# Two layers of a three-branch decoder trunk: the instruction order taken from the framework's other timing model

## The chip, the core and the metric

One core of a Trainium2 chip. The metric is device time in microseconds (us) of one execution. The core has five engines, each with a queue of its own: TensorE (PE in the profile, with its weight loads as PEld), VectorE (DVE), ScalarE (ACT), GpSimd (POOL), and SyncE (SP), which here only starts transfers. Each engine takes its instructions in the order of its queue; semaphores hold an instruction back until what it reads is written and what it overwrites has been read.

## What is computed

Two layers on a sequence of 512 tokens, width 1024, in fp32, and a final RMSNorm. Cut to what matters:

```python
def hybrid_layer(x, ...):
    h = rmsnorm(x, norm_g)
    proj = h @ w_in                       # 1024 x 8704: aq ak av az | u,v bz | cq ck cv cz | three gates
    ya = rmsnorm(diff_attention(rope(aq), rope(ak), av, lam), subln_g) * (1 - lam_init) * silu(az)
    uv = gelu(buv);  vb = layernorm(second half of uv)
    yb = u * (w_causal mixes vb over chunks of 128 + sgu_b) * silu(bz)
    yc = (softmax-weighted sum of three dilated windows of rope(cq), rope(ck), cv) * silu(cz)
    merged = sum over the branches of sigmoid(gate_n) * (y_n @ w_branch[n])
    return x + merged @ w_out
```

## The kernel before

**Arithmetic.** Every large product is made of three: weights and activations are each split into a rounded part ("hi") and the rest ("lo"), and TensorE adds hi x hi, lo x hi and hi x lo (lines 416 to 418, 439 to 441 and 452 to 454). Activations lie as tiles of 128 channels x 512 tokens. Some pairs of projections are made with seven products of half the length in place of eight (`seven`), for which sums and differences of weights are formed first (lines 178 to 181).

**Weights.** SyncE loads them in pieces of 128 x 1024 (`raw`, two buffers, line 140; a piece is loaded when an older one has been split). ScalarE rounds each half piece to `whi` (line 158, six buffers), and VectorE, or for each fifth half piece GpSimd, subtracts to get `wlo` (line 159, five buffers):

```python
        with tc.high_priority(offset=PRIO):
            A.activation(out=hi, in_=src, func=AF.Copy)
            (G if made[0] % LOMOD == 0 else V).tensor_tensor(out=lo, in0=src, in1=hi.bitcast(F32), op=ALU.subtract)
```

**Stages of a layer.** The head: products for `vb` (line 596 evicts them) and for A's values `va` (four PSUM banks, evicted by ScalarE, line 705), while VectorE scales x (line 585), splits it (`xh`, `xl`, line 422) and forms the mixed activations `mh`, `ml` (lines 505 to 508, split at 421 and 422). Then attention A and attention C, with other projections laid between their steps by hand (`fill`). Each q and k goes through `rope`: a VectorE shuffle (468) and product (469), a GpSimd product (470) and sum (471), a ScalarE rounding (732, 742) and a VectorE subtraction (733, 743). Each z is a SiLU: ScalarE's tanh (479) and a VectorE product (480). Then gates and branch products (`gl2`, `pb`), then the output product; its tail runs into the head of the next layer, or into the final norm.

**What sets the order.** The kernel's text gives each instruction a place; the splitting of weights is moved 300 places ahead by `high_priority`. When the tile framework closes its context, a list scheduler plays the whole program against a model of the core: whenever an engine is free in the model, it gets the ready instruction with the earliest place, and tile buffers are handed out as the model frees them. The order in which the model took the instructions becomes the order of each queue. Two such models exist, and the flag in the diff selects between them: a timeline of device occupancy (flag on), and the timing of the framework's functional simulator (flag off, the default). They differ in what they charge for instructions, transfers and semaphores; the program that they are given is the same. In the order that the first of them gave to the kernel before, 5508 of the 6605 instructions on TensorE's queue can be picked out as one run in written order; on VectorE's it is 747 of 1990, on ScalarE's 763 of 1662.

## Time and profile before

| | |
|---|---|
| time, median of 3 runs (lowest, highest) | 1154.71 us (1150.01, 1156.02) |
| the profiled execution: its own time | 1154.14 us |
| the profiled execution: span, first to last instruction | 1152.4 us |
| mean granted TensorE clock | 0.986 of full |
| busy: PE, PEld, DVE, ACT, POOL | 95%, 85%, 74%, 55%, 46% of the span |
| moved by DMA | 106.01 MB, mean 92 GB/s |

The profile is of one execution. Busy time is the time in which an engine's records lie; a matmul's record is longer than the distance to the next one's start, so a queue of matmuls reads as fully busy. Idle time is put down to the instruction that ended it. The span is 1.7 us shorter than the time of the same execution.

### The profile page before, as it was taken

How to read it: one execution, taken by the hardware profiler on the slowest of the kernel's cores; microseconds unless marked ns; L12 is line 12 of the kernel's file. 1: busy time of each engine (PE TensorE's matmuls, PEld its weight loads, DVE VectorE, ACT ScalarE, POOL GpSimd, SP SyncE). 2: the span in 40 equal slices, each digit the busy share in tenths (PEclk: the TensorE clock that was granted, in tenths of full speed). 3: DMA queues.
4: the chain of work that ended last, by engine and by line, in shares of the span. 5: the costliest groups of instructions: out<-in, count | busy, mean ns of one | idle time of the engine just before them, and what ended most of it. 6: DMA issues, size and time to landing. Idle time of an engine off the chain costs nothing.

```text
span 1152.4 us, 18434 instructions
## 1 busy us (share of the span) xinstructions
PE 1095.6 (95%) x6604; PEld 974.6 (85%) x6604; DVE 856.6 (74%) x1589; ACT 632.3 (55%) x1349; POOL 531.3 (46%) x503
## 2 busy tenths in 40 slices
PE   7898989999999999999997999899999999999977
PEld 5777879988888999988886888898888899999866
DVE  5796988667869887874569778857787887887533
ACT  5645666577865444443455475756777544544321
POOL 7653443235334667563342444323344456766312
PEclk9999999999999999999998999999999999999998
DMA  5221412220313333333622231313132233333333
GB/s 202 71 92 37 128 55 75 74 78 33 119 47 92 103 98 94 110 101 126 214 79 85 74 100 47 95 54 96 51 92 74 73 94 108 94 110 90 122 92 101
DMA packets 35643, 106.01 MB, mean 92 GB/s; under 512 B 4768, under 2 KB 8864, under 8 KB 35552
## 3 DMA queue, kind: packets, MB, share of 16 engines
q1 hardware_dynamic: 29936, 98.50, 27.5%
q10 hardware_dynamic: 5616, 6.34, 1.8%
q8 instruction: 52, 0.85, 0.3%
q14 instruction: 39, 0.32, 0.1%
HBM read 100.57 MB, written 4.24 MB: 91 GB/s over the span
## 4 chain that ended last, share of the span: by engine, by line
PE 68%; DVE 9%; issue 3%; DMA 2%; POOL 2%; ACT 2%; POOLq 0%; DVEq 0%; ACTq 0%; SPq 0%
PE ps_pj L416 11%; PE ps_pj L417 11%; PE ps_pj L418 11%; PE ps_to L416 7%; PE ps_to L418 7%; PE ps_to L417 7%; DVE wlo L159 2%; PE ps_to L898 2%; PE ps_to L1000 2%; DMA raw<-in_wpack 2%; PE ps_s L864 1%; PE ps_s L866 1%; PE ps_pj L441 1%; PE ps_pj L440 1%; PE ps_pj L439 1%
## 5 line engine op out<-in xcount | busy, mean ns | idle before, releaser
L158 ACT ACTIVATE whi<-raw 128x512 fp32r<-128x512 f32 x314 | 191.4, 626 | 225.8 <-DMA raw<-in_wpack 136.6
L159 DVE TENSOR_TENSOR wlo<-raw,whi 128x512 fp32r<-128x512 f32 x251 | 210.0, 844 | 88.1 <-ACT whi L158 44.2
L416 PE MATMUL ps_pj<-xh,whi 128*128 128x512 f32 (+1 forms) x544 | 208.4, 383 | 16.2 <-DVE z L480 7.1
L417 PE MATMUL ps_pj<-xl,whi 128*128 128x512 f32 (+1 forms) x544 | 205.3, 377 | 0.0
L418 PE MATMUL ps_pj<-xh,wlo 128*128 128x512 f32 (+1 forms) x544 | 204.4, 376 | 0.0
L159 POOL TENSOR_TENSOR wlo<-raw,whi 128x512 fp32r<-128x512 f32 x63 | 88.6, 1406 | 156.7 <-ACT whi L158 48.6
L416 PEld LDWEIGHTS ps_pj<-xh,whi 128*128 128x128 f32 x544 | 103.5, 190 | 35.6 <-DVE z L480 8.1
L418 PEld LDWEIGHTS ps_pj<-xh,wlo 128*128 128x128 f32 x544 | 103.6, 191 | 16.4
L417 PEld LDWEIGHTS ps_pj<-xl,whi 128*128 128x128 f32 x544 | 103.8, 191 | 15.6
L159 DVE TENSOR_TENSOR wlo<-t,whi 128x512 fp32r<-128x512 f32 x90 | 90.0, 1020 | 13.9 <-ACT whi L158 12.1
L158 ACT ACTIVATE whi<-t 128x512 fp32r<-128x512 f32 x112 | 64.8, 622 | 57.7 <-DVE t L179 29.6
L416 PE MATMUL ps_to<-mh,whi 128*128 128x256 f32 x320 | 91.0, 284 | 2.4 <-DVE zs L537 1.5
L417 PE MATMUL ps_to<-ml,whi 128*128 128x256 f32 x320 | 90.4, 283 | 0.0
L418 PE MATMUL ps_to<-mh,wlo 128*128 128x256 f32 x320 | 89.9, 283 | 0.2 <-DVE wlo L159 0.2
L470 POOL TENSOR_TENSOR rsh<-rsh,sinr 128x512 f32<-128x512 f32 x32 | 42.2, 1319 | 100.1 <-DVE rsh L468 100.1
L875 ACT ACTIVATE pr<-pr,nm 128x128 f32<-128x128 f32 (+3 forms) x128 | 71.0, 556 | 27.1 <-DVE nm L871 26.7
L871 DVE CUSTOM_DVE_ANT_0 pr<-ps_s,tab 128x128 f32<-128x128 f32 (+3 forms) x128 | 58.7, 483 | 14.7 <-PE ps_s L866 11.1
L416 PE MATMUL ps_to<-xh,whi 128*128 128x256 f32 x240 | 67.9, 283 | 0.4 <-ACT whi L158 0.4
L417 PE MATMUL ps_to<-xl,whi 128*128 128x256 f32 x240 | 67.9, 283 | 0.0
L418 PE MATMUL ps_to<-xh,wlo 128*128 128x256 f32 x240 | 67.8, 283 | 0.0
L416 PEld LDWEIGHTS ps_to<-mh,whi 128*128 128x128 f32 x320 | 61.3, 192 | 3.7 <-DVE zs L537 2.2
L790 POOL TENSOR_TENSOR acc<-acc,zs 128x512 f32<-128x512 f32 x32 | 51.0, 1601 | 23.3 <-DVE zs L789 19.5
(264 smaller groups left out, 3155.3 us busy)
## 6 DMA issues: line engine op xcount, KB each, us to landing
raw<-in_wpack SPq DMA_DIRECT2D x174, 512.0 KB
xf<-in_xT SPq DMA_DIRECT2D x8, 256.0 KB
xr<-in_xT ACTq DMA_DIRECT2D x8, 256.0 KB
x1d<-xf SPq DMA_DIRECT2D x8, 256.0 KB
xr<-x1d ACTq DMA_DIRECT2D x16, 128.0 KB
raw<-in_wpack SPq DMA_DIRECT2D x4, 256.0 KB
out<-xf SPq DMA_DIRECT2D x8, 128.0 KB
out<-xf ACTq DMA_DIRECT2D x8, 128.0 KB
```

Source lines behind the costliest of these rows:

```text
L158: A.activation(out=hi, in_=src, func=AF.Copy)
L159: (G if made[0] % LOMOD == 0 else V).tensor_tensor(out=lo, in0=src, in1=hi.bitcast(F32), op=ALU.subtract)
L416: T.matmul(ps, lhsT=wh, rhs=mh, start=first, stop=False)
L417: T.matmul(ps, lhsT=wh, rhs=ml, start=False, stop=False)
L418: T.matmul(ps, lhsT=wl, rhs=mh, start=False, stop=last)
L439: T.matmul(ps, lhsT=mh[:, ts], rhs=wh, start=kc == 0, stop=False)
L470: G.tensor_tensor(out=sh, in0=sh, in1=sinr, op=ALU.mult)
L790: G.tensor_tensor(out=acc[d], in0=acc[d], in1=th, op=ALU.add)
L871: V.tensor_tensor_reduce(out=pr[:, m, :W], in0=pss[m][:, :W], in1=tab[:, 0 if br == BR_A else 1, S - W :], op0=ALU.add, op1=ALU.min, scale ...
L875: A.activation(out=pr[:, m, :W], in_=pr[:, m, :W], func=AF.Exp, scale=-1.0, bias=nm[:, m : m + 1], accum_out=den[:, m : m + 1],)
L898: T.transpose(pt[:, j, :], pr[:, m, j * P : (j + 1) * P], ident)
L1000: T.matmul(po_[m][:, c], lhsT=v[:, j, 2 * h + m, :], rhs=pt[:, j, :], start=j + s_ == 0, stop=j == i and s_ == 1,)
```

## The change

The flag that selects the planner's timing model is turned off. No instruction, tile, buffer count, tensor or transfer in the kernel's text is changed; what may change is the order of the instructions on each queue, the buffer of a tag that each tile gets, and the semaphore waits that follow from both.

```diff
@@ -1132,7 +1132,7 @@
     args.append(nc.dram_tensor("out_0", (KC, P, S), F32, kind="ExternalOutput").ap())
-    with _tile.TileContext(nc, schedule_with_timeline_sim=True) as tc:
+    with _tile.TileContext(nc, schedule_with_timeline_sim=False) as tc:
         hybrid_kernel(tc, *args)
```

## Rows read from the trace of the kernel before

**Rows 1.** The page's head and its busy times by engine.

```profile
span 1152.4 us, 18434 instructions
PE 1095.6 (95%) x6604; PEld 974.6 (85%) x6604; DVE 856.6 (74%) x1589; ACT 632.3 (55%) x1349; POOL 531.3 (46%) x503
```

**Rows 2.** Windows by stage: stretch, length, busy PE PEld DVE ACT POOL, clock, DMA.

```profile
0.00:60.00 60.00, 48.73 (x186) 39.14 (x187) 38.89 (x63) 36.83 (x64) 43.24 (x68) 0.92 0.43 138
60.00:192.00 132.00, 121.99 (x650) 104.42 (x650) 114.38 (x246) 76.61 (x180) 58.16 (x50) 0.97 0.25 77
192.00:384.00 192.00, 188.46 (x1179) 168.32 (x1179) 146.58 (x306) 126.06 (x286) 73.70 (x87) 1.00 0.23 72
384.00:576.00 192.00, 190.59 (x1191) 172.66 (x1190) 138.90 (x189) 86.47 (x160) 108.05 (x76) 1.00 0.40 124
576.00:632.00 56.00, 49.66 (x212) 40.41 (x212) 44.90 (x63) 29.72 (x52) 19.66 (x14) 0.94 0.28 86
632.00:912.00 280.00, 274.28 (x1643) 242.24 (x1642) 210.50 (x488) 185.11 (x433) 110.41 (x120) 1.00 0.24 75
912.00:1086.00 174.00, 172.13 (x1170) 159.71 (x1170) 137.86 (x188) 77.98 (x148) 104.81 (x75) 1.00 0.34 104
1086.00:1152.00 66.00, 49.77 (x385) 47.73 (x383) 24.59 (x50) 13.49 (x29) 13.28 (x16) 0.93 0.30 93
```

**Rows 3.** Timeline of ScalarE at the head of layer 1: start, length, instruction.

```profile
625.32 0.63 ACT L421 ACTIVATE mh<-tm 128x512 fp32r<-128x512 f32 x1 [1.09 <-POOL tm L508]
625.86 0.67 ACT L705 ACTIVATE va<-ps_pj,rp 128x512 f32<-128x512 f32 x1
```

**Rows 4.** Timeline of TensorE there, ahead of its stop and behind it.

```profile
612.14 0.39 PE L453 MATMUL ps_pj<-whi,xul 128*128 128x512 f32 x1
...
612.37 0.39 PE L454 MATMUL ps_pj<-wlo,xuh 128*128 128x512 f32 x1
...
626.58 0.80 PE L416 MATMUL ps_pj<-xh,whi 128*128 128x512 f32 x1 [6.34 <-ACT va L705]
...
627.17 0.63 PE L417 MATMUL ps_pj<-xl,whi 128*128 128x512 f32 x1
627.60 0.63 PE L418 MATMUL ps_pj<-xh,wlo 128*128 128x512 f32 x1
```

**Rows 5.** Waits: who for whom, us in total, times, longest us.

```profile
ACT whi L158 <- DMA raw<-in_wpack: 136.6, 71, 8.4
POOL rsh L470 <- DVE rsh L468: 100.1, 25, 10.4
...
PE ps_pj L416 <- DVE z L480: 7.1, 3, 3.0
```

**Rows 6.** Groups by line and shape: busy us, mean ns, idle before.

```profile
L471 POOL TENSOR_TENSOR t<-t,rsh 128x512 f32<-128x512 f32 x30 | 41.5, 1382 | 2.9 <-DVE rd L880 1.4
L470 POOL TENSOR_TENSOR rsh<-rsh,sinr 128x512 f32<-128x512 f32 x32 | 42.2, 1319 | 100.1 <-DVE rsh L468 100.1
L732 ACT ACTIVATE q<-t 64x512 fp32r<-64x512 f32 x32 | 20.2, 631 | 11.8 <-POOL t L471 11.4
L178 POOL TENSOR_TENSOR t<-raw 128x512 f32<-128x512 f32 x28 | 37.4, 1336 | 35.2 <-DMA raw<-in_wpack 28.1 <-PE ps_to L898 6.9
```

**Rows 7.** Windows of line 471 alone, by stage: stretch, busy POOL, clock, DMA.

```profile
60.00:192.00 132.00, 11.29 (x8) 0.97 0.25 77
192.00:384.00 192.00, 10.36 (x8) 1.00 0.23 72
...
632.00:912.00 280.00, 22.41 (x16) 1.00 0.24 75
```

**Rows 8.** Windows of 4 us: a place with short stops, then the stop above.

```profile
80.00:84.00 4.00, 3.30 (x15) 2.47 (x14) 3.97 (x7) 0.22 (x1) 1.85 (x3) 1.00 0.32 67
...
624.00:628.00 4.00, 1.42 (x3) 1.17 (x4) 4.00 (x8) 2.61 (x6) 2.09 (x2) 0.51 0.45 131
628.00:632.00 4.00, 4.00 (x13) 3.21 (x12) 3.35 (x7) 1.77 (x5) 0.77 (x2) 0.64 0.43 131
```

**Rows 9.** Queue waits of SyncE: who for whom, us in total, times, longest us.

```profile
SPq L140 <- DVE wlo L159: 593.9, 108, 15.6
```

## Prediction

> **What bounds the kernel now.** I began with the page's head, to see which engine is near its limit, then took windows by stage, to see where that engine stops, and then the waits and the timeline at the largest stops.
>
> TensorE's records cover 1095.6 of the 1152.4 us, VectorE's 856.6 [rows 1]. The flag changes none of that work: the same matmuls have to pass, so an order can only give or take the time in which TensorE stands still or runs slowly. By stage [rows 2], TensorE stops for 11.3 us in the first 60 us (60 less 48.73) and for 16.2 us in the last 66 (66 less 49.77): the first loads, and the last products with the norm behind them. In between it stops for 10.0 + 3.5 + 1.4 + 6.3 + 5.7 + 1.9 = 28.8 us, in the order of the rows. The granted clock is below 1.00 in two of those stages: 0.97 over 132 us and 0.94 over 56 us, which is worth at most 4.0 + 3.4 = 7.4 us. So 36 us is all that an order can win between the ends.
>
> VectorE is the engine that TensorE waits behind when it waits. Its idle time in the same six stages is 17.6 + 45.4 + 53.1 + 11.1 + 69.5 + 36.1 = 232.8 us [rows 2]. It is 87% busy from 60 to 192 us, the tightest place, and 72 to 80% in the others.
>
> What a planner's order can do wrong is to be seen at the head of layer 1. TensorE stops for 6.34 us there and is let go by the eviction of `va` at 625.86 us [rows 3, 4]. The products that this eviction reads were over when the stop began, at about 620.2 us. It came late because ScalarE's queue holds a copy to `mh` ahead of it, and that copy waited for GpSimd's line 508 [rows 3]. An instruction that was ready stood behind one that was not. The planner puts an instruction where it is ready by the planner's times, so these must differ from the chip's here. The same is to be seen on GpSimd, at no cost to the end: it stands 100.1 us, at 25 places and for up to 10.4 us, with the product of `rope` at the head of its queue, waiting for VectorE's shuffle [rows 5].
>
> **What the change does, and what it costs.** It removes and adds no instruction, so no duration is added as such. It gives every queue another order. The cost is the sum of the waits in which a queue's head is not ready while something behind it is. The trace of before cannot show the other order, so I bound it.
>
> From below: nothing excludes a gain. If every stop between the ends went, it would be 1154.1 - 36 = 1118 us. I do not expect it, since a stop is gone only where the other model happens to be nearer to the chip.
>
> From above: the chains in which VectorE's next instruction depends on GpSimd. They are long, and a planner that takes GpSimd to be quicker than it is puts VectorE's instruction directly behind. Each q and k passes lines 470 (1.32 us) and 471 (1.38 us) on GpSimd and a rounding on ScalarE (0.63 us) before VectorE may subtract: 3.33 us [rows 6]. There are 32 of them (30 in the group shown, two in a smaller one), 8 from 60 to 192 us, 8 from 192 to 384 and 16 from 632 to 912 [rows 7]: 32 x 3.33 = 107 us. Each of the 28 groups of seven products has its first weight sum on GpSimd, 1.34 us [rows 6], ahead of VectorE's difference: 28 x 1.34 = 37 us. If every one of these stood uncovered and reached TensorE, it would be 107 + 37 = 144 us, or 1298 us.
>
> Which value between the ends? VectorE's idle time hides most of it. From 60 to 192 us there are 8 x 3.33 = 26.6 us of such waits against 17.6 us of idle time: 9 us are over and go to TensorE in full. From 192 to 384 it is 26.6 against 45.4, from 632 to 912 53.3 against 69.5, so both fit, and so do the weight sums. Idle time is not free either: today 232.8 us of it go with 28.8 us of stops of TensorE, one in eight. Hidden are 17.6 + 26.6 + 53.3 + 37 = 135 us, and an eighth is 17 us. Third, the head of a layer. I take one more stop of the kind shown there, for example in layer 0: 6.3 us, and behind it matmuls 0.43 us apart in place of 0.23 [rows 4]: 1.4 us at a granted clock of 0.51 and 4 us at 0.64 [rows 8], which is 0.7 + 1.4 = 2.1 us; together 8.4 us. The sum is 9 + 17 + 8 = 34 us. I take the full count of the chains because the trace gives no ground to leave some out, and the hidden price because that row is nearest: the stages concerned do have the idle time.
>
> The sum is made on the profiled execution, 1154.1 us, which is 1.7 us more than its span: 1188 us. The median of the runs is 0.6 us above that execution, and against it the forecast is 1189 us.
>
> The loads are part of what is reordered. SyncE has one queue of them, and its load of the next weight piece already waits for a `wlo` of VectorE at 108 places, 593.9 us in all [rows 9]: a `wlo` that is put behind another instruction delays a load, the rounding behind that load and the products behind both. What hides this today is the depth of six split half pieces. With twelve matmuls each at about 0.15 us (174 us over 1170 matmuls [rows 2]) six of them last 11 us. I cost it at nothing in the sum, and give it to a rival.
>
> The clock is where a rule speaks against the change. After the stop of 6.3 us the granted clock was 0.51 and then 0.64 in the next two windows, that is, the lower of the two levels, 1.2 GHz, for part of them; where TensorE stopped for 0.7 us in a window of 4 us it stayed at 1.00 [rows 8]. The Trainium skill, "TensorE: Matmul & The Clock Gate", section "HAM oscillation — how this bites in real kernels", says that idle gaps of TensorE bring the clock down, so that the restart is slow as well. The long stop agrees and the short ones show its limit. If all of the 26 us that I add outside the head's stop came as stops of 6.3 us, the slow restarts would add 26 / 6.3 x 2.1 = 9 us and the sum would be 1198 us; I take them as short ones, since the longest of the three waits for line 480, the largest such group apart from the head's, is 3.0 us [rows 5], and add nothing.
>
> **The rivals.** *Weights run dry.* Late `wlo`s delay loads until TensorE is out of weights. For it: the 593.9 us above, and ScalarE already stands at 71 places for a load, 136.6 us [rows 5]. Against it: from 192 to 576 us TensorE stops for 4.9 us in all, whatever the reason [rows 2], so the 11 us in hand do hide those waits. It decides from the point where a `wlo` is late by more than those 11 us. If half of the 71 waits lost their cover it would be 68 us: 1222 us.
>
> *Faster.* The other model puts the evictions of `va` ahead of the copies to `mh` at the layer's head. That alone ends the stop: 8.4 us. It would most likely come with a better order in the stage from 60 to 192 us, of whose 10.0 + 4.0 us I give it half, 7 us: 1154 - 15 = 1139 us. For it: today's order visibly has this fault, and the place is one pair of neighbours on one queue. Against it: it takes a model that is right where the present one is wrong, and not wrong elsewhere. It decides where `va` leaves PSUM within a microsecond of its last product.
>
> *No change.* Both planners go by the same written places, five in six of TensorE's instructions stand in written order today, and the projections are laid between the attention steps by hand. If the new queues differ only where nobody waits, it is 1154 us. Against it: VectorE and ScalarE have under half of their instructions in written order, so their order is the model's doing.
>
> **How the numbers follow.** I give the forecast (about 1161 to 1210 us) 0.52, weights that run dry (above that) 0.25, faster 0.13 and no change 0.10. Half a per cent, 5.8 us, is about what a measurement of this kernel can tell from no change. So slower has 0.52 + 0.25 = 0.77, same 0.10, faster 0.13. The predicted time is the likeliest case, 1189 us, with its own range of 1161 to 1210. For eight in ten the range goes down to the faster case, 1139 us, and up to the dry case on top of the forecast's own sum, 1154 + 34 + 68 = 1256 us; what lies outside is some 0.06 below (towards 1118) and 0.09 above (towards 1298).
>
> **What the profile after would show.** TensorE's busy time and count as before, 1095.6 us within some 10 us, with the added time as idle time ahead of matmuls. If the step on GpSimd's chains is right, VectorE's waits for lines 471, 732, 742 and 178 grow from a few us to tens, and the stages from 60 to 192 and 632 to 912 us lengthen while those with gates stay. If the head's step is right, one long stop stands in each layer's head, with the lower clock behind it. Dry weights would show as TensorE waiting for `whi` or `wlo`, and loads on the chain of waits. The prediction would be wrong if the stages with gates, where the seven products leave TensorE little to wait for, lengthen most; or if TensorE's busy time itself moved, by the clock or by records that stretch; or if VectorE's idle time grew and TensorE's did not.

## The result and the profile after

The changed kernel takes 1259.19 us (median of 4 runs, 1257.69 to 1262.17) against 1155.01 us of the kernel before beside it: a ratio of 1.0912, 95% interval 1.0888 to 1.0936, or 104 us more. The forecast was 1189 us with a range up to 1256: the direction was right, the size was three times the one forecast (104 us against 34).

The page's head and busy times after, to be held against [rows 1]:

```profile
span 1255.9 us, 18453 instructions
PE 1128.8 (90%) x6604; PEld 994.6 (79%) x6604; DVE 836.3 (67%) x1589; ACT 638.5 (51%) x1349; POOL 512.9 (41%) x503
```

The same instructions ran: the counts of every engine are those of before. TensorE stands still for 1255.9 - 1128.8 = 127.1 us, where it was 1152.4 - 1095.6 = 56.8: 70.3 us more. Its records also cover 33.2 us more, with the same 6604 matmuls. The two make up the 103.5 us by which the span grew. VectorE and GpSimd are less busy than before (by 20 and 18 us), ScalarE by 6 us more.

To see where, I cut both traces at the same instructions (the first scores product, the last product of the attention outputs, the first and last product of the gates' stage). Windows, first of before, then of after: stretch, length, busy PE PEld DVE ACT POOL with counts, granted clock, DMA. In each fence the first four rows are layer 0 (the head up to the first scores product, attention A, attention C, gates), the last three are layer 1 without its head.

```profile
0.00:87.70 87.70, 74.23 (x294) 59.59 (x295) 66.50 (x109) 50.12 (x88) 58.27 (x79) 0.94 0.37 120
87.70:222.90 135.20, 127.39 (x787) 114.01 (x785) 107.73 (x249) 80.10 (x203) 51.06 (x46) 0.97 0.23 71
222.90:365.00 142.10, 138.77 (x826) 121.89 (x824) 108.81 (x234) 100.04 (x225) 57.49 (x72) 1.00 0.24 75
365.00:534.10 169.10, 167.49 (x1115) 154.36 (x1116) 132.25 (x182) 76.64 (x145) 102.16 (x73) 1.00 0.35 107
...
650.20:776.70 126.50, 123.13 (x782) 110.48 (x782) 96.15 (x245) 77.80 (x197) 49.47 (x46) 1.00 0.23 72
776.70:918.30 141.60, 138.37 (x826) 121.89 (x824) 110.34 (x235) 100.65 (x226) 57.19 (x70) 1.00 0.25 75
918.30:1085.60 167.30, 166.31 (x1121) 154.16 (x1122) 131.56 (x181) 75.70 (x144) 99.22 (x72) 1.00 0.34 105
```

```profile
0.00:98.50 98.50, 69.27 (x265) 54.68 (x265) 64.58 (x108) 49.61 (x87) 52.15 (x79) 0.88 0.34 107
98.50:253.50 155.00, 137.89 (x810) 122.59 (x811) 104.78 (x250) 82.76 (x202) 49.52 (x46) 0.92 0.20 62
253.50:408.30 154.80, 142.54 (x805) 121.74 (x804) 109.42 (x241) 100.64 (x226) 52.12 (x70) 0.98 0.23 69
408.30:580.70 172.40, 168.13 (x1128) 156.11 (x1127) 123.62 (x175) 76.35 (x143) 100.09 (x74) 0.99 0.31 102
...
701.70:853.70 152.00, 136.44 (x806) 120.89 (x807) 103.62 (x248) 82.42 (x201) 51.31 (x47) 0.94 0.19 60
853.70:1008.60 154.90, 142.70 (x805) 121.90 (x804) 105.90 (x240) 101.10 (x227) 51.18 (x68) 0.98 0.23 69
1008.60:1182.80 174.20, 168.45 (x1128) 156.03 (x1127) 121.13 (x176) 76.66 (x143) 98.75 (x74) 0.99 0.31 100
```

Attention A grew by 19.8 and 25.5 us, attention C by 12.7 and 13.3, the gates by 3.3 and 6.9; the two heads and the two output stages have the other 22.0. Layer 1's attention A is the telling pair of rows: TensorE stopped there for 126.5 - 123.1 = 3.4 us, and now for 15.6; and it is busy for 13.3 us longer, with the granted clock at 0.94 in place of 1.00. A part of that is work that moved: the counts show 24 matmuls more in this stage and 21 fewer in attention C behind it (23 more and 21 fewer in layer 0).

The 70.3 us of new idle time of TensorE are spread like this (length less busy time, by stage): 39.4 in the four attention stages, 21.4 in the two heads (13.5 to 29.2 us in layer 0, 6.3 to 12.0 in layer 1), 9.5 in the gates and the output stages.

Who waits for whom (us in total, times, longest). Before, rows that did not stand ahead of the prediction:

```profile
ACT q L732 <- POOL t L471: 11.4, 14, 2.0
...
ACT kh L742 <- POOL t L471: 9.3, 7, 2.8
...
DVE t L179 <- POOL t L178: 12.1, 8, 2.3
...
DVE kl L743 <- ACT kh L742: 6.2, 10, 1.8
```

After:

```profile
ACT whi L158 <- DMA raw<-in_wpack: 87.5, 44, 4.4
...
ACT kh L742 <- POOL t L471: 52.3, 14, 8.4
...
DVE t L179 <- POOL t L178: 38.3, 26, 2.3
...
DVE kl L743 <- ACT kh L742: 36.7, 23, 4.3
...
ACT q L732 <- POOL t L471: 31.1, 16, 4.1
...
PE ps_pj L416 <- DVE z L480: 21.4, 4, 8.6
...
PE ps_pj L416 <- ACT va L705: 15.6, 2, 9.2
...
PE ps_to L454 <- POOL wlo L159: 10.9, 1, 10.9
```

ScalarE's roundings of q and k stand at the head of its queue for 83.4 us, waiting for GpSimd's last step of `rope`; before it was 20.7. The loads did not run dry: ScalarE's wait for them fell from 136.6 us [rows 5] to 87.5. Yet the longest stop of the whole trace, 10.9 us up to 30.3 us in layer 0's head, is a wait for a weight's low half. Its rounding was done by 18.2 us; the subtraction stood behind small operations of 32 columns on GpSimd's queue until 29.0 us, before until 21.8.

The longest stop in an attention stage shows how it works. Timelines from 181 to 196 us: GpSimd, ScalarE, VectorE, TensorE (start, length, instruction, idle time before it and what ended it).

```profile
184.32 1.30 POOL L470 TENSOR_TENSOR rsh<-rsh,sinr 128x512 f32<-128x512 f32 x1 [0.76 <-DVE rsh L468]
185.57 1.72 POOL L180 TENSOR_TENSOR t<-raw 128x512 f32<-128x512 f32 x1
187.26 1.26 POOL L181 TENSOR_TENSOR t<-raw,t 128x512 f32<-128x512 f32 x1
188.47 1.26 POOL L471 TENSOR_TENSOR t<-t,rsh 128x512 f32<-128x512 f32 x1
```

```profile
189.77 0.63 ACT L742 ACTIVATE kh<-t 64x512 fp32r<-64x512 f32 x1 [8.37 <-POOL t L471]
190.30 0.61 ACT L158 ACTIVATE whi<-t 128x512 fp32r<-128x512 f32 x1
...
193.75 0.59 ACT L479 ACTIVATE th<-ps_pj 128x512 f32<-128x512 f32 x1
```

```profile
194.37 0.69 DVE L480 SCALAR_TENSOR_TENSOR z<-th,ps_pj 128x512 f32<-128x512 f32 x1 [0.73 <-ACT th L479]
```

```profile
184.64 0.40 PE L418 MATMUL ps_pj<-xh,wlo 128*128 128x512 f32 x1
...
186.16 0.28 PE L417 MATMUL ps_pj<-xl,whi 128*128 128x256 f32 x1
186.28 0.28 PE L418 MATMUL ps_pj<-xh,wlo 128*128 128x256 f32 x1
195.11 0.58 PE L416 MATMUL ps_pj<-xh,whi 128*128 128x256 f32 x1 [8.55 <-DVE z L480]
195.49 0.42 PE L417 MATMUL ps_pj<-xl,whi 128*128 128x256 f32 x1
195.71 0.41 PE L418 MATMUL ps_pj<-xh,wlo 128*128 128x256 f32 x1
```

Read it from the bottom. TensorE needs a bank of `ps_pj` and waits for `z`; `z` waits for the tanh `th`. The products that `th` reads were over at about 185.0 us, but `th` ran at 193.75, since ScalarE's queue has a `kh` ahead of it, and seven more entries behind that `kh`, which ran from 190.30 to 193.75 us. That `kh` waited 8.37 us for line 471, which came behind two weight sums in GpSimd's queue; 4.7 us of this wait fell behind 185.0 us, where `th` was ready. The four operations of GpSimd took 1.30 + 1.72 + 1.26 + 1.26 = 5.5 us; the planner with the flag off charges four times 0.43, 1.7 us. So up to 3.8 us of the delay are the price; the rest is the place of the `kh` ahead of the tanh, and what had gathered behind it.

### The profile page after: what moved, and what is told of

The parts are those of the page before. It is cut to its first block, busy times and chain, and to the rows that moved or that the text cites. A ratio compares the mean times of both kernels' runs of the same rounds, so it can differ in the third digit from the quotient of the medians.

```text
span 1255.9 us, 18453 instructions
## 1 busy us (share of the span) xinstructions
PE 1128.8 (90%) x6604; PEld 994.6 (79%) x6604; DVE 836.3 (67%) x1589; ACT 638.5 (51%) x1349; POOL 512.9 (41%) x503
## 3 DMA queue, kind: packets, MB, share of 16 engines
q10 hardware_dynamic: 5616, 6.34, 1.6%
## 4 chain that ended last, share of the span: by engine, by line
PE 32%; DVE 7%; POOL 5%; ACT 5%; issue 3%; DMA 2%; POOLq 0%; ACTq 0%; DVEq 0%; SPq 0%
PE ps_pj L416 5%; PE ps_pj L417 5%; PE ps_pj L418 4%; PE ps_to L416 4%; PE ps_to L418 4%; PE ps_to L417 4%; DMA raw<-in_wpack 2%; DVE wlo L159 1%; ACT pr L875 1%; POOL acc L790 1%; ACT whi L158 1%; POOL t L471 1%; PE ps_s L864 1%; PE ps_pj L439 1%; PE ps_s L866 1%
## 5 line engine op out<-in xcount | busy, mean ns | idle before, releaser
L158 ACT ACTIVATE whi<-raw 128x512 fp32r<-128x512 f32 x314 | 193.0, 626 | 190.6 <-DMA raw<-in_wpack 87.5
L416 PE MATMUL ps_pj<-xh,whi 128*128 128x512 f32 (+1 forms) x544 | 216.4, 398 | 38.8 <-DVE z L480 21.4
L159 DVE TENSOR_TENSOR wlo<-raw,whi 128x512 fp32r<-128x512 f32 x251 | 195.0, 780 | 74.9 <-PE ps_pj L418 31.0
L416 PEld LDWEIGHTS ps_pj<-xh,whi 128*128 128x128 f32 x544 | 106.1, 195 | 57.6 <-DVE z L480 22.1
L417 PEld LDWEIGHTS ps_pj<-xl,whi 128*128 128x128 f32 x544 | 106.5, 196 | 14.2
L159 DVE TENSOR_TENSOR wlo<-t,whi 128x512 fp32r<-128x512 f32 x90 | 84.4, 943 | 18.1 <-PE ps_pj L418 7.8
L179 DVE TENSOR_TENSOR t<-t,raw 128x512 f32<-128x512 f32 x28 | 42.9, 1532 | 38.3 <-POOL t L178 38.3
```

Of the source, the lines that this page charges most:

```text
L179: SE[1].tensor_tensor(out=s2, in0=s1, in1=a11, op=ALU.subtract)
L416: T.matmul(ps, lhsT=wh, rhs=mh, start=first, stop=False)
L417: T.matmul(ps, lhsT=wh, rhs=ml, start=False, stop=False)
```

## The experiments

Two facts of the planner are at hand. With the flag off it charges GpSimd 0.833 ns a column, 0.43 us for 128x512, where the traces show 1.3 to 1.6 us. And it charges TensorE's matmuls two to three and a half times as much behind a pause. Both are constants that can be set before the kernel is planned; none of them alters an instruction.

All times are medians beside the kernel before on the same chip. TensorE's idle time is the span less its busy time; stops are gaps of over 3 us between matmuls, counted in the trace.

| run | us | ratio, 95% interval | TensorE idle | TensorE busy | clock | stops: number, us |
|---|---|---|---|---|---|---|
| before | 1155.0 | 1 | 56.8 | 1095.6 | 0.986 | 3, 12.6 |
| after | 1259.2 | 1.0912 (1.0888 to 1.0936) | 127.1 | 1128.8 | 0.956 | 12, 67.2 |
| off_pool_priced | 1182.8 | 1.0235 (1.0208 to 1.0263) | 71.2 | 1108.3 | 0.979 | 4, 20.0 |
| off_pool_dear | 1174.0 | 1.0162 (1.0134 to 1.0191) | 68.8 | 1100.0 | 0.985 | 3, 22.3 |
| off_no_ramp | 1258.4 | 1.0897 (1.0862 to 1.0932) | 128.8 | 1127.3 | 0.954 | 12, 68.4 |
| off_both | 1179.7 | 1.0211 (1.0187 to 1.0236) | 71.5 | 1108.2 | 0.975 | 4, 25.1 |
| on_pool_cheap | 1196.9 | 1.0361 (1.0331 to 1.0390) | 84.7 | 1109.6 | 0.973 | 5, 31.2 |
| on_jitter | 1153.5 | 0.9988 (0.9973 to 1.0004) | 53.3 | 1096.8 | 0.983 | 3, 14.1 |
| off_pool_vec | 1231.5 | 1.0663 (1.0635 to 1.0691) | 102.0 | 1128.1 | 0.960 | 8, 44.6 |
| on_va_first | 1150.1 | 0.9955 (0.9940 to 0.9970) | 52.5 | 1094.4 | 0.981 | 4, 19.7 |
| off_va_first | 1260.9 | 1.0925 (1.0894 to 1.0956) | 128.6 | 1129.9 | 0.954 | 13, 69.0 |
| on_va_lead | 1149.1 | 0.9941 (0.9917 to 0.9965) | 53.6 | 1094.5 | 0.986 | 4, 15.9 |
| off_act_on | 1240.8 | 1.0732 (1.0694 to 1.0769) | 106.9 | 1132.1 | 0.962 | 7, 41.1 |
| on_act_off | 1204.9 | 1.0427 (1.0365 to 1.0490) | 93.9 | 1114.5 | 0.965 | 7, 42.0 |
| off_dve_on | 1247.2 | 1.0795 (1.0757 to 1.0832) | 118.8 | 1125.3 | 0.971 | 7, 44.2 |
| off_pe_on | 1241.4 | 1.0740 (1.0702 to 1.0777) | 118.9 | 1120.4 | 0.955 | 10, 54.5 |
| off_pool_on | 1264.5 | 1.0938 (1.0909 to 1.0966) | 126.0 | 1138.5 | 0.948 | 15, 69.8 |
| off_ad_on | 1217.2 | 1.0518 (1.0483 to 1.0553) | 93.6 | 1122.1 | 0.976 | 7, 37.7 |
| off_adp_on | 1205.1 | 1.0435 (1.0397 to 1.0474) | 81.7 | 1128.5 | 0.972 | 7, 26.5 |
| off_all_on | 1154.8 | 0.9994 (0.9976 to 1.0011) | 52.9 | 1095.6 | 0.983 | 4, 17.7 |

### Which price is it

`off_pool_priced`, in the changed kernel (the second constant keeps the price of starting a transfer, which hangs on the first, as it was):

```diff
+    from concourse import hw_specs as _hw
+
+    _hw.TRN2Spec.CYCLE_T = {**_hw.TRN2Spec.CYCLE_T, mybir.EngineType.Pool: 2.6}
+    _hw.TRN2Spec.DMA_START_POOL_CYCLES_HWDGE = 160.26
```

> The changed kernel, with the planner charging GpSimd about 1.33 us for a 128x512 operation, near what the trace shows (1.32 and 1.38 us), in place of the 0.43 us that it charges there now. Theory G (the loss comes from GpSimd being priced at a third of its time, so that its consumers are put at the head of a queue too early): most of the 104 us comes back, 1155 to 1190 us, and ScalarE's waits for line 471 at 742 and 732 (52.3 and 31.1 us) fall under 30 us together. Theory R (the planner's extra charge on TensorE's matmuls after a pause spoils the order): little changes, 1235 to 1270 us. Theory N (neither of the two prices): 1235 to 1270 us.

`off_no_ramp`, and `off_both` with both edits:

```diff
+    _hw.TRN2Spec.PE_CYCLE_PSTATE_LOW = _hw.TRN2Spec.PE_CYCLE
+    _hw.TRN2Spec.PE_CYCLE_PSTATE_MID = _hw.TRN2Spec.PE_CYCLE
```

> The changed kernel, with the planner charging every 512-column matmul the same, also behind a pause of TensorE, where it charges twice to three and a half times as much now. Theory R: most of the 104 us comes back, 1155 to 1190 us. Theory G and theory N: 1235 to 1270 us, with ScalarE still waiting some 80 us for line 471.

> Both prices altered at once. Theory G: as the first of these runs, within 15 us, 1155 to 1190 us. Theory R: as the second, 1155 to 1190 us with the first one near 1259. If both matter, this one is clearly the fastest of the three. Theory N: 1235 to 1270 us.

`on_pool_cheap`, in the kernel before:

```diff
+    _hw.TRN2Spec.CYCLE_T = {**_hw.TRN2Spec.CYCLE_T, mybir.EngineType.Pool: 0.18}
```

> The kernel before (the flag on) with the one price made wrong: GpSimd's 128x512 operations are charged about 0.43 us, as in the changed kernel's planner. Theory G: it loses most of what the flag loses, 1215 to 1270 us, with ScalarE's waits for line 471 grown from 20.7 us to 60 or more. Theories R and N: within 1 per cent of the kernel before, 1145 to 1166 us.

GpSimd's right price alone gives back 1259.2 - 1182.8 = 76 of the 104 us; the charge behind pauses does nothing. With the right price no stop for `z` is over 3 us any more, and the 10.9 us stop is gone. The two stops for `va` stay (5.6 and 7.4 us, 13.0 for 15.6), so they are not the price's doing. ScalarE's waits for line 471 in `off_pool_priced`, and in `on_pool_cheap`:

```profile
ACT kh L742 <- POOL t L471: 16.9, 10, 3.0
...
ACT q L732 <- POOL t L471: 7.3, 6, 1.8
```

```profile
ACT kh L742 <- POOL t L471: 48.2, 14, 7.7
ACT q L732 <- POOL t L471: 31.6, 16, 4.8
```

They fall to 24.2 us and rise to 79.8, as theory G has it. The time follows only in part: with the flag on the cheap price costs 43 us, not the 60 to 115 expected, although these waits are as long as in the changed kernel (83.4). So their sum is a sign of the fault and not its cost.

`off_pool_dear` prices GpSimd at 2.0 us per 128x512:

```diff
-    _hw.TRN2Spec.CYCLE_T = {**_hw.TRN2Spec.CYCLE_T, mybir.EngineType.Pool: 2.6}
-    _hw.TRN2Spec.DMA_START_POOL_CYCLES_HWDGE = 160.26
+    _hw.TRN2Spec.CYCLE_T = {**_hw.TRN2Spec.CYCLE_T, mybir.EngineType.Pool: 3.9}
+    _hw.TRN2Spec.DMA_START_POOL_CYCLES_HWDGE = 106.84
```

> The changed kernel with GpSimd priced half as much again as in the first experiment, about 2.0 us for a 128x512 operation, where the trace shows 1.3 to 1.6. If the order follows how near the price is to the trace: 1195 to 1225 us, between the cheap price and the right one. If it is the cheap side alone that hurts (a consumer placed too early blocks a queue, one placed late only leaves room): 1165 to 1190 us.

Too dear is no worse than about right (1174.0 against 1182.8 us); too cheap costs 76 us more. In this kernel it is the cheap side that hurts.

### Is it luck, or other prices

`on_jitter`, in the kernel before, a price 4% lower (0.80 for 0.833 in the constant), and `off_pool_vec`, on top of `off_pool_priced`:

```diff
+    key = bass.MemoryType.SB, mybir.EngineType.DVE
+    _hw.TRN2Spec.ACCESS_CYCLES = {**_hw.TRN2Spec.ACCESS_CYCLES, key: 308}
```

> The kernel before (flag on), its planner charging GpSimd 4 per cent less: a price as good as the old one that still shuffles the queues, as a control. Theory L (luck: the kernel's other constants were chosen with one order in view, and any other order loses 20 us or more, so that the 23 to 26 us left with GpSimd priced rightly, and part of the 43 us of the cheap price, are that): 1172 to 1200 us. Theory P (prices: an order is as good as its prices): within 1 per cent of before, 1143 to 1166 us.

> The changed kernel with GpSimd priced as in the first experiment, and with VectorE's operations that read SBUF charged 0.26 us more (a 128x512 one 0.85 us, as the trace shows for the weights' low halves, in place of 0.59). Theory P: most of the 26 us left goes, 1150 to 1172 us. Theory L: no clear gain, 1170 to 1200 us.

The 4% is a real shuffle: by the traces, at least 342 of TensorE's instructions, 141 of VectorE's, 130 of ScalarE's and 17 of GpSimd's stand out of the order of before (897, 468, 326 and 61 in the changed kernel). It moved the time by nothing that can be told. So it is not so that any other order loses 20 us. A like shuffle with the flag off was not run. But theory P failed as well: with VectorE charged the mean that the trace shows for the `wlo`, the order got worse by 49 us. The 0.26 us were added to every operation of VectorE that reads SBUF, also to those of one column, which take 0.15 us (line 922): nearer to the trace for the `wlo`, further from it for the small ones. No one wait stands out there: TensorE's six longest groups of waits have 5.9 to 13.2 us each, and six different releasers. A flat price is not right for these operations (last section), but whether this is why was not shown. A price nearer to the trace for one large group did not make a better order here.

### The layer's head

`on_va_first` and `off_va_first` put all eight copies to `mh` behind the evictions of `va`:

```diff
-                    A.activation(
+                    last_va[0] = A.activation(
...
-            mixes(blocks)
+            with tc.issue_after(last_va[0].ins):
+                mixes(blocks)
```

> The kernel before (flag on) with one order forced: at each layer's head ScalarE evicts va ahead of all copies to mh. Theory H (the layer head's stop is worth what the prediction gave it, 6.3 us and 2.1 us of slow clock): 1143 to 1150 us, and no stop of TensorE over 3 us for va. Theory L: the queues behind it shuffle, and it comes out at 1165 us or more.

> The same forced order in the changed kernel, where the two stops for va measure 6.4 and 9.2 us. Theory H: these 15.6 us go, and some 5 us of slow clock behind them: 1235 to 1245 us. If the heads' delay is covered further on, or the shuffle decides: 1255 us or more.

The stop did not go. In layer 1 of `on_va_first`, ScalarE and then TensorE:

```profile
621.78 0.63 ACT L158 ACTIVATE whi<-raw 128x512 fp32r<-128x512 f32 x1 [5.32 <-DMA raw<-in_wpack]
622.32 1.25 ACT L707 ACTIVATE va<-ps_pj,rp 128x512 f32<-128x512 f32 x2
```

```profile
623.04 0.79 PE L416 MATMUL ps_pj<-xh,whi 128*128 128x512 f32 x1 [7.07 <-ACT va L707]
```

With `mh` out of the way, a weight rounding that waits for its load stands ahead of `va` (now line 707), and the stop is 7.07 us for 6.34. The 5 us that this version wins come from elsewhere in the new order. With the flag off it wins nothing, and the two stops are 4.3 and 8.7 us for 6.4 and 9.2. `on_va_lead` puts the last two roundings behind `va` too:

```diff
+                for w in whis[-2:]:
+                    tc.add_manual_dep(w.ins, last_va[0].ins.name, ..., reason="va leads")
```

> Flag on; va at each layer's head ahead of the copies to mh and of the last two weight roundings too, since with mh out of the way a rounding that waited 5.3 us for its load stood in front. If that is what is left of the stop, its 7.1 us and some 2 us of slow clock go: 1139 to 1145 us. If the delayed roundings cost as much: 1148 to 1156 us.

```profile
620.37 0.50 PE L416 MATMUL ps_pj<-xh,whi 128*128 128x512 f32 x1 [1.23 <-ACT va L707]
```

Now the stop is 1.23 us, and the granted clock stays at 1.00 behind it. In the 32 us that follow, 3.3 us of new stops appear (windows of 12.00 and 20.00 us with TensorE busy for 10.00 and 18.66; in `on_va_first` the same windows are full). From the first product of layer 1's head to its first scores product it is 75.5 us before, 75.4 in `on_va_first` and 70.5 in `on_va_lead`; from there to the end of the span 502.2, 501.0 and 504.0. So the stop was worth 5 us where it stood, and some 2 to 3 of them were given back. What is left is within what executions of one kernel differ by (1150.0 to 1156.0 us before), and the time is that of `on_va_first` within what can be told. Both versions are about half a per cent faster than the kernel before; they are the fastest of the study.

### Which queue carries it

Here the program is planned twice. The first plan's order of one or more queues is laid on the second as a chain; the other queues are planned around it. The code shown is that of ScalarE's queue from before in the changed kernel; `on_act_off` has the two flags the other way round, and the others name other queues.

```diff
+    nc, pos = trace(True)
+    order = [pos[i.name] for b in nc.cur_f.blocks for i in b.instructions if i.engine == Q and i.name in pos]
+    nc, _ = trace(False, Q, order)
...
+                for a, b in zip(order, order[1:]):
+                    tc.add_manual_dep(mine[b], mine[a].name, ..., reason="queue order")
```

> The changed kernel (flag off) with ScalarE's queue alone held to the order of the kernel before; the other queues are planned with the flag off around it. Theory S (ScalarE's queue carries the loss: an eviction or a rounding that waits for GpSimd holds up everything behind it): 1155 to 1190 us. Theory M (every queue carries its part): 1195 to 1235 us. If ScalarE's queue matters little: 1240 to 1265 us.

> The converse: flag on, ScalarE's queue alone held to the order of the changed kernel. Theory S: 1225 to 1265 us. Theory M: 1175 to 1225 us. If ScalarE's queue matters little: 1150 to 1170 us.

> The changed kernel with VectorE's queue alone held to the order of the kernel before. Theory S: 1230 to 1265 us. Theory M: 1195 to 1235 us. If VectorE's queue is the carrier, as the prediction's argument over VectorE's idle time has it: 1155 to 1190 us.

> The changed kernel (flag off) with TensorE's queue alone held to the order of the kernel before. Theory T (TensorE's own order carries what ScalarE's and VectorE's do not: it puts a matmul in front whose input the planner takes to be ready): 1155 to 1200 us. Theory J (no queue alone carries it; each of them, planned with the cheap GpSimd, keeps enough entries that wait): 1230 to 1262 us.

> The changed kernel with GpSimd's queue alone held to the order of the kernel before. If GpSimd's own order is the carrier: 1155 to 1200 us. Theory J: 1245 to 1265 us, since GpSimd has the fewest instructions and the most idle time.

> The changed kernel with ScalarE's and VectorE's queues both held to the order of the kernel before. Alone they gave back 18 and 12 us. Theory J: together more than the sum, 1170 to 1210 us. Theory T: about the sum, 1222 to 1240 us.

> As the run before, and GpSimd's queue held too: only TensorE's matmuls and the loads are planned with the flag off. Theory J: 1155 to 1175 us. Theory T: 1215 to 1240 us, and TensorE then waits for instructions that run at the times of the kernel before.

> The flag off, with the queues of TensorE, ScalarE, VectorE and GpSimd all held to the order of the kernel before; only the loads' issue on SyncE is planned with the flag off. If the order of the four engines is all that the flag alters: 1149 to 1162 us. If the loads' places or anything else that the flag does matter: 1170 us or more.

Theory S fails: ScalarE's queue in the old order gives back 18 us, VectorE's 12, TensorE's 18, GpSimd's nothing (5 us worse): 43 of the 104 us, if one adds them. ScalarE's and VectorE's together give 42, which is more than 18 + 12; with GpSimd's 54. The last 50 need TensorE's order as well, and with all four held the time is that of before (0.9994). So the order of those four queues is all that the flag alters in the time, the places of the loads do nothing, and no queue carries the loss alone. The two runs with two and three queues held (1217.2 and 1205.1 us) fell between the ranges of theories J and T, into neither. The converse, `on_act_off`, costs 49 us (its four runs are 1199.6, 1199.6, 1210.1 and 1212.8 us), in theory M's range: a bad order of ScalarE's queue does more harm than the good one repairs. A queue in a good order still waits for the others: in `off_pe_on` ScalarE waits 70.2 us for line 471 at `kh` and `q`.

## Why the prediction was wrong in size

**What held.** The work is unchanged and the time came in as idle time of TensorE and as matmuls at a low clock. VectorE's waits grew as named (line 742 from 6.2 to 36.7 us, line 178 from 12.1 to 38.3). The layer's head has a long stop for `va` in both layers, 6.4 and 9.2 us, where I had added one of 6.3: the stops for `va` grew by 9.3 us. The gates stayed within 2 and 4%. The cause put ahead, a planner that takes GpSimd to be quicker than it is, is shown for 76 of the 104 us by the price alone.

**The step that failed: "VectorE's idle time hides most of it".** It gave 9 + 17 us for chains whose sum was 144, and with the 6.3 us at the head 32 us of stops; measured are 70.3. Term by term: 26 us put for the chains, 39.4 measured in the attention stages and 9.5 in the gates and output stages; 6.3 put for the heads, 21.4 measured. The first 60 us, where the 10.9 us stop came, had no term at all. Layer 1's attention, where 53.3 us of waits were to fit into 69.5 us of idle time at a price of an eighth, lengthened by 25.5 + 13.3 us. The step took VectorE for the queue that waits, and idle time for cover. Neither is so. Of the waits for GpSimd the largest is that of ScalarE's rounding of k (52.3 us), and what it holds back (in the stop shown, a tanh) is what releases TensorE's bank. Idle time elsewhere in the stage does not cover a stop of 8 us: TensorE has two banks of `ps_pj`, each filled by 24 matmuls at 0.23 us [rows 4]; while one is held, the other gives it 5.5 us of work at most (an estimate). Idle time is not the right measure of cover; how long TensorE can run on the banks that it has is. The stop at layer 1's head, from which the argument began, was also read too simply: between 620.2 and 625.9 us ScalarE waited for line 508 for 1.09 us and for VectorE's line 507 for 1.05, and for the other 3.5 us it worked on entries that stood ahead of `va`.

**The term that was mis-sized: the clock.** I put 2.1 us. TensorE is busy 33.2 us longer, where the prediction allowed some 10 and named more as a sign of being wrong. The granted clock of the whole span is 0.956 for 0.986, which is 0.044 x 1255.9 - 0.014 x 1152.4 = 39 us at most, since part of it falls into the stops. Behind the stop shown above, in windows of 4 us (columns as in the windows above):

```profile
184.00:188.00 4.00, 2.56 (x17) 2.00 (x15) 2.16 (x4) 0.00 (x0) 3.68 (x3) 1.00 0.00 2
188.00:192.00 4.00, 0.00 (x0) 0.00 (x0) 0.68 (x1) 2.21 (x4) 1.73 (x2) 0.55 0.78 255
192.00:196.00 4.00, 0.89 (x4) 0.89 (x5) 2.98 (x5) 3.08 (x8) 0.00 (x0) 0.50 0.02 7
196.00:200.00 4.00, 4.00 (x23) 4.00 (x23) 1.51 (x8) 1.72 (x5) 0.00 (x0) 0.67 0.00 0
```

The clock falls to the lower of its levels, 1.2 GHz, while TensorE stands, and it restarts slowly: matmuls of 256 columns are 0.21 us apart at 195.5 us, where they were 0.12 apart at 186.2. Low for 2.6 us of the last window (0.67 over 4 us, at half the full clock), so until about 198.7 us, this stop costs some (198.7 - 195.1) / 2 = 1.8 us on top, near the 2.1 that I read from [rows 4, 8].

Over the whole trace, TensorE is busy for 75.0 us at the lower level, before for 24.9. At half the clock that is a loss of 37.5 against 12.4 us: 25 of the 33. The clock fell 18 times while work was left, before 6 times, and 37.5 / 18 and 12.4 / 6 are both 2.1 us. So the price was right and the number was wrong. "I take them as short ones" failed twice over: there are 12 stops over 3 us in place of 3, and shorter ones brought the clock down too. The trace of before had a case: a stop of 1.78 us that ended at 107.68 us (windows of 4 us):

```profile
104.00:108.00 4.00, 2.22 (x15) 1.84 (x14) 2.25 (x7) 3.94 (x11) 2.31 (x3) 1.00 0.00 0
108.00:112.00 4.00, 4.00 (x24) 4.00 (x23) 1.71 (x4) 0.88 (x3) 0.00 (x0) 0.58 0.00 0
```

The rule that I set aside, the Trainium skill, "TensorE: Matmul & The Clock Gate", section "HAM oscillation — how this bites in real kernels" (idle gaps bring the clock down, and the restart is slow), agrees with these rows; taking it at its word gave 1198 us, still too low, since the number of stops was.

The other 8 us stay open: TensorE's busy time less the loss to the clock is 1083 us before and 1091 after, and over the runs it lies between 1081 (`off_pe_on`) and 1102 (`off_dve_on`).

**The rivals.** *Weights run dry* did not come as thought: ScalarE's wait for loads fell by 49 us, and the one long wait of TensorE for a weight, 10.9 us, was for GpSimd's subtraction and not for a load. *Faster* rested on `va` ahead of `mh`. Forced with the flag on, that leaves the stop in place, with a rounding in front of it; with both moved, the stop goes, and of the 5 us that this wins at the head some 2 to 3 are given back behind it. The 8.4 us that I gave to that stop are not to be had in full by moving `va`.

**What stays open.** With GpSimd priced near the trace, 20 to 29 us are left over the kernel before (`off_pool_dear`, `off_pool_priced`). The two planners also differ in what they charge for matmuls, transfers and semaphores; none of these but the charge behind pauses was tried. Nor was a price with a fixed part: by the column, a GpSimd operation of 32 columns is charged 32 x 2.6 ns = 0.08 us in `off_pool_priced`, and the trace has them at 0.25 to 0.8 us. The stops for `va`, 13.0 us, are a part of what is left.

## What to carry to other kernels

Before you trust a planner's order, hold its price for each engine against the profile's mean duration; here one price at a third of the true one was worth 76 us, and one half as much again too dear cost nothing more. Cost a late instruction by what stands behind it in its queue and how long TensorE can run without that, not by the idle time of the engine that waits. Count also how often TensorE will stop, and not only for how long: each fall of the clock cost 2.1 us on top here. A stop at the head of a stage is worth its length only if nothing behind it is waiting to take its place: ending one of 7 us won 5 us at the head, and about half of them were lost again behind it.

## What the hardware showed unexpectedly

VectorE's subtraction of two tiles in SBUF takes 0.69 us when GpSimd is idle, and up to 1.8 us when it starts while GpSimd is at work on two tiles there. Timelines of GpSimd and VectorE in the changed kernel. VectorE's first row runs while GpSimd is idle, the second while it runs line 471 (177.29 to 178.90 us), the third, which reads PSUM, while it runs line 470 (184.32 to 185.62 us):

```profile
177.29 1.61 POOL L471 TENSOR_TENSOR t<-t,rsh 128x512 f32<-128x512 f32 x1
```

```profile
172.43 0.69 DVE L159 TENSOR_TENSOR wlo<-raw,whi 128x512 fp32r<-128x512 f32 x1 [1.47 <-ACT pT L921]
...
177.68 1.77 DVE L159 TENSOR_TENSOR wlo<-raw,whi 128x512 fp32r<-128x512 f32 x1
...
184.74 0.67 DVE L943 TENSOR_TENSOR on<-ps_to,r 128x512 f32<-128x512 f32 x1
```

The second ends 0.55 us after GpSimd's operation does, nearly a whole length later. It is no single case: of the 73 `wlo` subtractions that began while GpSimd ran an operation of 512 columns, 71 ended 0.54 to 0.64 us after that operation; the 212 beside an idle GpSimd took 0.66 to 0.70 us. The Trainium skill, "SBUF — State Buffer", section "SBUF: two separate sides", calls the ports that the two share an exclusive lock that whoever starts first holds for the whole instruction, VectorE taking part when both inputs lie in SBUF; these rows agree. A planner with one price for that operation (0.59 us here) cannot know whether it will be 0.69 or 1.77.
